# Row halves in turn, transposes, an RMS root on ScalarE and held LayerNorm sums in a two-layer hybrid decoder step

## The chip, the cores and the metric

The kernel runs on one core of a Trainium2 chip. A core has TensorE (PE, with its weight loads as PEld), VectorE (DVE), ScalarE (ACT) and GpSimd (POOL), and SyncE (SP), which here only issues DMAs. The metric is the device time of one execution in microseconds; the median of several runs counts.

## The reference, cut to what matters

One step of a decoder with two layers, in fp32: 1024 new tokens of one prompt, and 32 sample tokens (8 sequences of 4) with states of their own. A layer is a projection `x @ w_in`, three groups of mixers side by side (6 heads RWKV-7, 5 heads GLA, 5 heads RetNet, 64 values to a head), an output projection with LayerNorm, then a gated feed-forward part with a convolution of width 3 over the tokens, and again LayerNorm:

```python
p = x @ w_in[l]
p_rw, p_gl, p_rt = _split(p, (RWKV_COLS, GLA_COLS, RET_COLS))
y_a, sh, s_a = _rwkv7_mix(p_rw, ...)
y_b, s_b = _gla_mix(p_gl, ...)          # ends in _rms_heads(o) * norm_w * silu(g)
y_c, s_c = _ret_mix(p_rt, ...)          # ends in _rms_heads(o) * silu(g)
mix = jnp.concatenate([y_a, y_b, y_c], axis=-1) @ w_out[l]
x = _layer_norm(ALPHA * x + mix, ...)
f, cv = _conv_ffn(x, ...)               # (gelu(a) * b) @ w_down
x = _layer_norm(ALPHA * x + f, ...)
```

with `_rms_heads(o) = o * rsqrt(mean(o * o, -1) + 1e-6)` for each head and token. RWKV's recurrence over tokens (a state of 64 x 64 per head, decayed, corrected and added to) is worked out in chunks of 64 tokens, which takes products within a chunk and the inverse of a unit triangular matrix.

## The kernel before, in words

**Tokens and operands.** The 1056 tokens stand in three blocks `NB` of 384, 384 and 288 columns, channels in the partitions; the third holds the 32 sample tokens and the last 256 of the prompt. Each fp32 weight and activation of the large products is split in a high and a low part (`split`: the high part by a copy on ACT, the low part by a subtraction on POOL), and `mm3` makes three matmuls of each product (high with high, high weight with low activation, low weight with high activation). Small products in the mixers are plain fp32 matmuls, which the trace shows as two instructions each. All matmuls are issued by line L128, all transposes by L131, so groups of the profile are told apart by their tiles.

**Order on TensorE.** A planner, `Tensor`, keeps its instructions in the order in which they are written out. `run` takes streams (generators) and fillers: each burst of a stream ends with a `yield` of the time after which its next burst is expected to have its operands, from the hand-set table `AFTER`; while no stream is ready by the planner's own clock, the filler's matmuls are written out. The engine then follows this order, ready or not: where a time in the table is too short, the engine waits at that burst with the filler behind it. The other engines' orders come from the program's order and the framework's scheduler.

**A layer's stages** (layer 0 / layer 1 in us of the trace):

- First projection tiles and small operands (0 to 95 / 1690 to 1830). `group_a` makes RWKV's 12 M-tiles `pa` of each block by `gemm_steps`, with weights that come in pieces of 256 KB through a `Feed`, `MS = [2, 0, 1, ...]` first.
- RWKV (95 to 590 / 1830 to 2285). For batches `s.b` of 128 tokens (two chunks), eight in a layer, and the samples: `rwkv_front` makes the operands (two small projections `zw`, `za` of 64 rows each, with `sh` from the rows 0 to 63 and 64 to 127), `rwkv_gram` the products within chunks (tile `gps`, operands `ra`, `bk`; a head is 64 rows, a pair of heads 128), `rwkv_tok` the token-major operands (tiles `tv`, `tb`), `rwkv_solve` the triangular inverse on DVE with transfers `gd`, `ud` (lines L630, L632), `rwkv_merge` the joining of its blocks (tiles `xps`, `tps`, copy `x11` at L656), `rwkv_core` the chunk after chunk recurrence (`sp`, `zy`, `up`). Filler is `pa`, and then `group_b`, the projection `gt` for GLA and RET in token tiles.
- GLA, RET and the output projection (590 to 930 / 2285 to 2640). For each of nine token tiles `gla_front`, `gla_back`, `ret_front`, `ret_back`; each back ends in `finish`, which makes the RMS norm and the gate. `out_proj` makes the tiles `po`, adds the residual, and takes LayerNorm's sums as it goes; `LayerNorm.stats` ends them by two matmuls `lnm`, `lnv` and a root by Ln and Exp (L956, L957), `LayerNorm.steps` applies them (subtraction L965, multiplication L966, scale L967) and splits the result into `x1`.
- Feed-forward (930 to 1690 / 2640 to 3385). `up_blocks(0, ...)` makes the first pair of tiles (`wU0` and `wU22`) block by block, since `x1` of the third block comes last; after it `up` and `down` for the other tiles. `up_conv` brings a tile `pu` through the convolution.

The PSUM pool `pm` (tag "m") has two banks for all small RWKV products, `front` in the GLA and RET stage gives banks of a shared tag, and `pd` holds the banks "d" of the down projection.

In `rwkv_gram` each head of the pairs has a bank and a burst of its own:

```python
for j0, j1 in ((0, 2), (2, 3)):
    for h in range(2):
        hs = slice(h * 64, h * 64 + 64)
        gps = pmt("gps")[:, 0:(j1 - j0) * 256].rearrange("p (j c t) -> p j c t", j=j1 - j0, c=2)
```

In `finish` the root is `rsqrt`: 12 small DVE operations on tiles `nw` (128 x 5) by Newton's steps (L242 to L248).

Of the kernel before, what the change touches and what calls it, by code (L numbers as in the profile page):

```python
# [14 lines left out]
ALU = mybir.AluOpType  # L15
# [19 lines left out]
# expected times (us) from a step to what it makes ready  # L35
AFTER = {"key": 5.93, "sh": 3.5, "rkv": 2.0, "block": 6.0, "blockin": 2.5, "x": 3.0, "operands": 8.0, "gram": 0.9, "tv": 0.9, "tb": 0.9, "solve": 24.0, "ud": 4.5, "joined": 4.0, "mask": 1.5, "gd": 4.5, "x11": 1.28, "x21": 1.4, "x22": 0.6, "z": 1.4, "s": 1.58, "am": 2.0, "sx": 1.0, "sout": 3.0, "y": 7.3, "gate": 1.4, "state": 2.5, "done": 7.0, "turn": 2.5, "tokin": 3.36, "ev": 2.25, "gexp": 2.6, "gqt": 1.6, "rrot": 5.5, "rqt": 2.0, "at": 2.5, "qm": 0.8, "vx": 0.9, "gstate": 1.2, "tk": 4.5, "gateout": 4.0, "yin": 2.2, "yout": 4.5, "gnext": 1.2, "rout": 8, "rnext": 0.8, "yt": 0.5, "yready": 1.79, "ln": 3.0, "lnk": 1.5, "lns": 3.0, "ln1": 3.0, "ln2": 9.0}
# [18 lines left out]
# constant columns  # L55
# [10 lines left out]
class Event:  # L66
    """A time on the tensor engine from which something it has to wait for is expected."""
# [7 lines left out]
class Stream:  # L75
    """Work on the tensor engine in bursts: yields the time (us) until the next one can start, or an Event or a condition."""
# [24 lines left out]
class Tensor:  # L101
    """The tensor engine, its instructions kept in the order of the program, with an estimate of its time (us)."""

    def __init__(self, tc, engine):
        self.tc, self.engine, self.t, self.last, self.posts = tc, engine, 0.0, None, []
        Event.clock = self.clock
# [4 lines left out]
    def order(self, ins, cols, passes):  # L111
        ins = ins.ins
# [20 lines left out]
    def post(self, after, do):  # L133
        """Calls `do` when the time has come: a store that would hold up its queue before."""
# [7 lines left out]
    def run(self, streams, filler):  # L142
        """Emits the streams, the first ready one first, and the filler where none is; ends with the streams."""
# [14 lines left out]
def step_kernel(ctx: ExitStack, tc: tile.TileContext, xT, wA, wB, wO, wU, wD, pp, pb, lora, bg, bgk, shT, cvT, srw, sgl, srt,  # L158
# [27 lines left out]
    def split(dst_h, dst_l, src, le=None):  # L186
        """The two parts of src; returns the instructions."""
        return A.copy(dst_h, src), (le or G).tensor_tensor(dst_l, src, dst_h.bitcast(F32), ALU.subtract)  # L188
# [14 lines left out]
    class Feed:  # L203
        """Weights in two parts, piece after piece ([P, k, c] each), as far ahead as there is room."""
# [28 lines left out]
        def k(self, first, k):  # L233
            """The parts of row k of the matrix whose first piece is `first`, and whether its piece ends with it."""
# [3 lines left out]
    def rsqrt(pl, x, mul, add):  # L238
        """1 / sqrt(x * mul + add), by Newton's steps from the exponent's half."""
# [16 lines left out]
    def xtiles(what, n):  # L256
        """The two parts of a block; before the high part of the third one there is room for the low parts of its samples."""
# [4 lines left out]
    def gemm_ch(w, xs, n, name):  # L262
        """One M-tile of channel-major output over block n."""
        ps = pg.tile([P, 512], F32, tag="g", name=name)[:, :NB[n][1]]
# [1411 lines left out]
```

## Time and profile before

| | |
|---|---|
| median of 3 runs | 3442.24 us (3440.7 to 3452.11) |
| span of the profiled execution | 3430.9 us |
| the median over this span | 11.3 us more |
| busy: PE, DVE, ACT, POOL | 93%, 60%, 42%, 39% |
| mean granted clock of TensorE | 0.952 |
| layer 0: RWKV; GLA, RET and output projection; feed-forward | 95 to 590; 590 to 930; 930 to 1690 us |
| layer 1: the same | 1830 to 2285; 2285 to 2640; 2640 to 3385 us |
| last LayerNorm | 3385 to 3431 us |
| DMA | 288.24 MB, mean 84 GB/s |

The profiled execution's only time is its span; the runs are timed from outside it. PE's busy share counts matmuls whose ends are modelled and that overlap, so where one burst ends is read from the start of the next one. A wait in square brackets is idle time of the engine ahead of that instruction, with what ended it. "PE gps L128 <- DVE bk L533" reads: TensorE, about to start a matmul into gps, waited for DVE's write of bk.

### The profile page before, as it was taken

To read this page: it belongs to the slowest core of one execution; us is meant where nothing else is said; L and a number is where in the kernel's file an instruction comes from. 1 tells how busy PE (TensorE), PEld (TensorE's weight loads), DVE (VectorE), ACT (ScalarE), POOL (GpSimd) and SP (SyncE) were. 2 spreads that over 40 slices of the span, in tenths; PEclk is the share of its full clock that TensorE was granted. 3 is DMA by queue.
4 is the path that set the end of the run, shared out by engine and by line. 5 is a ranking of instruction groups with operands and counts; after the bars stand their busy time and mean duration, and the time that the engine had idled before them with its cause. 6 is when DMAs were issued, how large, how long until landed. Compare 5 with 4: busy or idle time off the path is not lost.

```text
span 3430.9 us, 59397 instructions
## 1 busy us (share of the span) xinstructions
PE 3198.4 (93%) x22110; PEld 2975.9 (87%) x22110; DVE 2068.6 (60%) x5037; ACT 1434.7 (42%) x3208; POOL 1332.6 (39%) x1660
## 2 busy tenths in 40 slices
PE   9889999988899999999888999999788999999995
PEld 8778888776799999999877888887777999999995
DVE  3577565776756544454746866646777564545457
ACT  6554332334543334333575543323346423333335
POOL 5443222224553334333565522221336433433345
PEclk9789999998999999999998999999989999999998
DMA  7333213433311111111154432234433111111111
GB/s 249 112 110 99 79 54 102 139 115 102 106 60 47 44 44 50 50 44 50 56 164 140 133 91 68 63 128 119 129 94 100 48 44 44 56 44 44 44 44 56
DMA packets 233261, 288.24 MB, mean 84 GB/s; under 512 B 65212, under 2 KB 146908, under 8 KB 232972
## 3 DMA queue, kind: packets, MB, share of 16 engines
q1 hardware_dynamic: 223852, 271.98, 26.3%
q10 hardware_dynamic: 9120, 12.47, 1.2%
q8 instruction: 173, 2.83, 0.4%
q14 instruction: 116, 0.95, 0.1%
HBM read 225.94 MB, written 58.43 MB: 83 GB/s over the span
## 4 chain that ended last, share of the span: by engine, by line
PE 70%; DVE 16%; DMA 4%; ACT 4%; issue 3%; POOL 2%; SPq 1%; ACTq 0%; DVEq 0%; POOLq 0%
PE pu L128 27%; PE pd L128 13%; PE gt L128 9%; PE pa L128 5%; PE po L128 3%; DVE tm L630 2%; DVE U L632 2%; PE zy L128 2%; PE gps L128 2%; PE rop L128 1%; DVE c L1401 1%; PE gop L128 1%; POOL wil L188 1%; DMA N<-gd 1%; DVE s L940 1%
## 5 line engine op out<-in xcount | busy, mean ns | idle before, releaser
L1401 DVE SCALAR_TENSOR_TENSOR c<-u,ppt,c 128x32 f32<-128x32 f32 (+1 forms) x704 | 395.8, 589 | 545.5 <-ACT c L1392 523.8
L188 POOL TENSOR_TENSOR wil<-wir,wih 128x512 fp32r<-128x512 f32 (+1 forms) x264 | 366.3, 1395 | 365.8 <-ACT wih L188 361.2
L128 PE MATMUL gt<-wih,xh 128*128 128x320 f32 (+1 forms) x1008 | 340.1, 339 | 0.9 <-DVE mx L388 0.9
L1448 DVE TENSOR_TENSOR acc<-acc,pd 128x384 f32<-128x384 f32 (+1 forms) x480 | 247.7, 518 | 139.5 <-PE pd L128 137.5
L128 PE MATMUL gt<-wil,xh 128*128 128x320 f32 (+1 forms) x1008 | 316.1, 315 | 6.5 <-POOL wil L188 5.2
L128 PE MATMUL gt<-wih,xl 128*128 128x320 f32 x896 | 281.6, 314 | 0.0
L188 ACT CAST wih<-wir 128x512 fp32r<-128x512 f32 (+1 forms) x296 | 185.6, 637 | 162.4 <-PE po L128 71.5
L128 PE MATMUL pa<-xh,wih 128*128 128x384 f32 (+1 forms) x576 | 216.5, 376 | 20.4 <-DVE mx L388 11.8
L630 DVE TENSOR_TENSOR tm<-U,N 96x60 f32<-96x60 f32 (+24 forms) x558 | 179.1, 321 | 69.9 <-DMA N<-gd 48.4
L128 PEld LDWEIGHTS gt<-wih,xh 128*128 128x128 f32 (+1 forms) x1008 | 187.5, 186 | 38.6 <-issue 21.9
L128 PE MATMUL pa<-xl,wih 128*128 128x384 f32 (+1 forms) x576 | 201.4, 350 | 3.3 <-POOL xl L188 3.0
L128 PE MATMUL pa<-xh,wil 128*128 128x384 f32 (+1 forms) x576 | 200.7, 348 | 3.6 <-POOL wil L188 2.2
L128 PEld LDWEIGHTS gt<-wil,xh 128*128 128x128 f32 (+1 forms) x1008 | 188.5, 187 | 10.2 <-POOL wil L188 9.1
L188 POOL TENSOR_TENSOR hl<-c,hh 128x384 fp32r<-128x384 f32 x132 | 128.1, 971 | 159.6 <-ACT hh L188 133.0
L632 DVE TENSOR_TENSOR U<-U,tm 96x60 f32<-96x60 f32 (+24 forms) x558 | 170.3, 305 | 14.0
L128 PEld LDWEIGHTS gt<-wih,xl 128*128 128x128 f32 x896 | 173.1, 193 | 0.0
L1392 ACT ACTIVATE c<-pu,ppt 128x384 f32<-128x384 f32 (+1 forms) x264 | 172.8, 655 | 0.0
L1380 ACT COPY u<-pu 128x384 f32<-128x384 f32 x176 | 84.1, 478 | 195.2 <-PE pu L128 195.1
L188 ACT CAST hh<-c 128x384 fp32r<-128x384 f32 x132 | 64.4, 488 | 222.4 <-DVE c L1407 222.3
L128 PEld LDWEIGHTS pa<-xh,wih 128*128 128x128 f32 x576 | 119.7, 208 | 35.1 <-DVE mx L388 13.2
L128 PE MATMUL po<-yh,wih 128*128 128x384 f32 (+1 forms) x384 | 138.9, 362 | 9.1 <-DVE ac L1325 6.7
L128 PE MATMUL po<-yh,wil 128*128 128x384 f32 (+1 forms) x384 | 131.7, 343 | 3.7 <-DVE wil L188 3.7
(810 smaller groups left out, 9862.6 us busy)
## 6 DMA issues: line engine op xcount, KB each, us to landing
wir<-in_wA_dram SPq DMA_DIRECT2D x144, 256.0 KB
wir<-in_wO_dram SPq DMA_DIRECT2D x96, 256.0 KB
wir<-in_wB_dram SPq DMA_DIRECT2D x56, 320.0 KB
tokd<-ev SPq DMA_DIRECT2D x112, 160.0 KB
x<-rkvd SPq DMA_DIRECT2D x16, 576.0 KB
tk<-tokd SPq DMA_DIRECT2D x16, 480.0 KB
rkvd<-mx SPq DMA_DIRECT2D x36, 192.0 KB
tk<-tokd SPq DMA_DIRECT2D x16, 400.0 KB
```

Of the source, the lines that this page charges most:

```text
L128: self.order(self.engine.matmul(out, lhsT, rhs, start=start, stop=stop), cols, 4 if rhs.dtype == F32 else 1)
L188: return A.copy(dst_h, src), (le or G).tensor_tensor(dst_l, src, dst_h.bitcast(F32), ALU.subtract)
L630: V.tensor_tensor(tm, U[:, 0:nr, i:i + 1].to_broadcast([4 * ns, nr, 31 - i]), N[:, i:i + 1, i + 1:32].to_broadcast([4 * ns, nr, 31 - i]), ...
L632: V.tensor_tensor(U[:, 0:nr, i + 1:32], U[:, 0:nr, i + 1:32], tm, ALU.add)
L940: self.ends["V"] = V.tensor_tensor(self.s1, acc[0] if k == 1 else self.s1, acc[k], ALU.add)
L1380: A.copy(u[:, 2:386], ps)
L1392: A.activation(c[:, :W], ps, AF.Identity, scale=pc(PP_CV + 4 * t + 2), bias=pc(PP_CV + 4 * t + 3))
L1401: V.scalar_tensor_tensor(cv, src, pc(PP_CV + 4 * t + tap), cv, ALU.mult, ALU.add)
L1448: V.tensor_tensor(acc[n][m], acc[n][m], ps, ALU.add)
```

## The change

It has seven parts. (1) Small matmuls on 64 rows are written out so that rows 0 to 63 and rows 64 to 127 alternate, each half into a bank of its own: `zw` and `za` in `rwkv_front`; the two heads of a pair in `rwkv_gram`, whose four bursts of a batch become two; and RET's products `rsp`, which took all 128 rows with zeroed copies of the other head before. For these the two scaled copies to `qT` on ACT become part of one copy. (2) `rwkv_tok` makes `tv` (and the samples' `tb`) by transposes instead of matmuls with the identity. (3) `finish` takes the root on ACT by Ln and Exp, with a table load for the set that has both, kept behind Square; the 12 DVE operations go. (4) The first two `pa` tiles of block 0 in a layer are made together, k by k. (5) The third block's LayerNorm sums are built as before but written out (`TE.hold`) only behind the two feed-forward tiles of block 0, and these two take banks of `pd`. (6) In `LayerNorm.steps`, with a split asked for, the odd channels' multiplication goes to POOL and the low part's subtraction to DVE; even channels stay as they were. (7) `AFTER["x11"]` goes from 1.28 to 3.0, and the operands of batches 0 and 1 get 5.5 more.

```diff
-"x11": 1.28,
+"x11": 3.0, "early": 5.5,
...
+    def hold(self, do):
+        self.held = []
+        do()
+        held, self.held = self.held, None
+        return lambda: [self.order(*h) for h in held]
...
+    def gemm_two(feed, first, xs, n, names):
+        ps = [pg.tile([P, 512], F32, tag="g", name=name)[:, :NB[n][1]] for name in names]
+        xh, xl, _ = xs[n]
+        for k in range(KD):
+            for i, p in enumerate(ps):
+                h, lo, _ = feed.k(first + 2 * i, k)
+                mm3(p, h, lo, xh[:, k], xl[:, k], k == 0, k == KD - 1)
+            for _ in range({3: 1, 7: 3}.get(k, 0)):
+                feed.free()
+            if k < KD - 1:
+                yield 0
+        return ps
...
-            for i, z in enumerate((zw, za)):
-                for j in range(NPAIR):
+            for j in range(NPAIR):
+                for i, z in enumerate((zw, za)):
...
-            yield AFTER["operands"]
+            yield AFTER["operands"] + (AFTER["early"] if s.b < 2 else 0)
...
                 for j0, j1 in ((0, 2), (2, 3)):
+                    gps = [pmt("gps")[:, 0:(j1 - j0) * 256].rearrange(...) for _ in range(2)]
+                    for j in range(j0, j1):
+                        for c in range(2):
+                            for h in range(2):
+                                hs = slice(h * 64, h * 64 + 64)
+                                TE.matmul(gps[h][:, j - j0, c], bk(j, c)[hs], ra(j, c)[hs], start=True, stop=True)
                     for h in range(2):
-                        hs = slice(h * 64, h * 64 + 64)
-                        gps = pmt("gps")[:, 0:(j1 - j0) * 256].rearrange(...)
-                        for j in range(j0, j1):
-                            for c in range(2):
-                                TE.matmul(gps[:, j - j0, c], bk(j, c)[hs], ra(j, c)[hs], start=True, stop=True)
-                        V.tensor_tensor(g5[:, j0:j1, :, h], gps, ...)
-                        yield AFTER["gram"]
+                        V.tensor_tensor(g5[:, j0:j1, :, h], gps[h], ...)
+                    yield 2 * AFTER["gram"]
...
-                TE.matmul(tv[:W, j * P:(j + 1) * P], s.v[:, j], ident, start=True, stop=True)
+                TE.transpose(tv[:W, j * P:(j + 1) * P], s.v[:, j], ident)
...
-                    (V if hl or k % 2 else G).tensor_tensor(a, a, s2, ALU.mult)
+                    ((G if k % 2 else V) if hl else (V if k % 2 else G)).tensor_tensor(a, a, s2, ALU.mult)
...
-                        for ins, e in zip(split(hl[0][:, k], hl[1][:, k], a), "AG"):
+                        for ins, e in zip(split(hl[0][:, k], hl[1][:, k], a, V if k % 2 else G), "AV" if k % 2 else "AG"):
...
-            A.activation(sq, dst, AF.Square)
+            first = A.activation(sq, dst, AF.Square)
...
-            sm = rsqrt(gp_, sm, 1.0 / 64, 1e-6)
+            ins = TE.after(A.preload_act_table_set("natural_log_exp_and_others"), first)
+            TE.after(A.activation(sm, sm, AF.Ln, scale=1.0 / 64, bias=eps(1, rows)), ins)
+            A.activation(sm, sm, AF.Exp, scale=-0.5)
...
-            A.copy(qT[:, 0:2], tp[:, 0:2 * rows].rearrange("p (g t) -> p g t", g=2))
-            for h in range(2):
-                A.activation(qT[:, 2 + h:6:2], tp[:, 2 * rows:4 * rows].rearrange(...), AF.Copy, scale=C("h2")[:, h:h + 1])
+            A.copy(qT[:, 0:4], tp[:, 0:4 * rows].rearrange("p (g t) -> p g t", g=4))
...
+            sp = [front("rsp")[:rows, 0:(3 - i) * rows].rearrange(...) for i in range(2)]
             for h in range(4):
-                TE.matmul(sp[:rows, h * rows:(h + 1) * rows], qT[:, 2 + h], qT[:, h // 2], start=True, stop=True)
+                hs = slice((h % 2) * 64, (h % 2) * 64 + 64)
+                TE.matmul(sp[h % 2][:, h // 2], qT[hs, 2 + h // 2], qT[hs, h // 2], start=True, stop=True)
...
-            ln.stats()
+            if n < 2:
+                ln.stats()
+            else:
+                stats3.append(TE.hold(ln.stats))
...
+            ps = gemm_ch(w, x1, n, f"pu{t}", None if t % NJ or n else pd.tile([P, 512], F32, tag="d", name="pu"))
...
+                if n == 0 and j == 0:
+                    stats3[0]()
```

Three places show how the order moves. The first is TensorE in layer 0, at the first gram of the first batch; `pa` with `xh`, `xl` (the activation's parts) and `wih`, `wil` (the weight's parts) is filler. Before:

```order
L128 MATMUL gps<-ra,bk 128x128 x4
L128 MATMUL pa_1_1084<-xh_222,wih_1009 128x384
L128 MATMUL pa_1_1084<-xl_223,wih_1009 128x384
L128 MATMUL pa_1_1084<-xh_222,wil_1008 128x384
L128 MATMUL pa_1_1084<-xh_222,wih_1009 128x384
L128 MATMUL pa_1_1084<-xl_223,wih_1009 128x384
L128 MATMUL pa_1_1084<-xh_222,wil_1008 128x384
L128 MATMUL gps<-ra,bk 128x128 x4
```

Two bursts of four matmuls, each in one bank, with six filler matmuls between them. After, with the numbers of the buffers:

```order
L138 MATMUL pa7_1_1134<-xh1_210,wil36_1051 128x384
L138 MATMUL gps_1155<-ra_898,bk_899 128x128
L138 MATMUL gps_1156<-ra_898,bk_899 128x128
L138 MATMUL gps_1155<-ra_898,bk_899 128x128
L138 MATMUL gps_1156<-ra_898,bk_899 128x128
L138 MATMUL gps_1155<-ra_898,bk_899 128x128
L138 MATMUL gps_1156<-ra_898,bk_899 128x128
L138 MATMUL gps_1155<-ra_898,bk_899 128x128
L138 MATMUL gps_1156<-ra_898,bk_899 128x128
L138 MATMUL pa7_1_1134<-xh1_210,wih37_1071 128x384
```

The eight stand in one burst and alternate between two banks; the first of them is now the 460th matmul of the program, and was the 429th; the first gram of batch 1 goes from the 569th to the 642nd.

The second is ACT at the first `finish` of a GLA tile in layer 0; `yg` is the tile's result, `rsq` its squares, `rsm` their sums by head, `ev` an eviction of the filler's bank `gt`, `upe` one of the state's update. Before:

```order
L981 COPY yg<-gop 128x320
L983 ACTIVATE rsq<-yg 128x320
L876 COPY ev<-gt 128x320
L1076 ACTIVATE upe<-gup,eb 128x64
L1076 ACTIVATE upe<-gup,eb 32x64
```

After:

```order
L1012 COPY yg<-gop 128x320
L1014 ACTIVATE rsq<-yg 128x320
L1018 ACT_TABLE_LOAD
L1019 ACTIVATE rsm<-rsm,cs 128x5
L1020 ACTIVATE rsm<-rsm 128x5
L904 ACT_TABLE_LOAD
L904 ACTIVATE ev<-gt 128x320
L1110 ACTIVATE upe<-gup,eb 128x64
```

Between the squares and the two evictions stand a table load, Ln on what DVE has summed, Exp and a second table load. The program has 118 table loads after the change and had 65; 36 of them are at L1018.

The third is TensorE where layer 0's feed-forward part begins; `po` is the output projection's last tile, `pu` the up projection's tiles with the activation parts `x1h`, `x1l`. Before:

```order
L128 MATMUL po_10249<-yh_9555,wih_10207 128x288
L128 MATMUL po_10249<-yl_9556,wih_10207 128x288
L128 MATMUL po_10249<-yh_9555,wil_10206 128x288
L128 MATMUL lnm<-s_9920,cs 128x288
L128 MATMUL lnv<-s_9921,cs 128x288
L128 MATMUL pu_10404<-x1h_9250,wU0h_10382 128x384
L128 MATMUL pu_10404<-x1l_9251,wU0h_10382 128x384
```

After:

```order
L138 MATMUL pu<-x1h_9166,wU22h_10166 128x384
L138 MATMUL pu<-x1l_9167,wU22h_10166 128x384
L138 MATMUL pu<-x1h_9166,wU22l_10165 128x384
L138 MATMUL lnm<-s_9686,cs 128x288
L138 MATMUL lnv<-s_9687,cs 128x288
L138 MATMUL pu_10240<-x1h_9676,wU0h_10148 128x384
L138 MATMUL pu_10240<-x1l_9677,wU0h_10148 128x384
```

The two LayerNorm matmuls stood right behind the last `po`; now the 48 matmuls of both tiles of block 0 stand ahead of them, and block 1's tiles behind them.

More of the change, by code (lines that the diff above doesn't have):

```diff
@@ L104, in __init__ @@
     def __init__(self, tc, engine):
-        self.tc, self.engine, self.t, self.last, self.posts = tc, engine, 0.0, None, []
+        self.tc, self.engine, self.t, self.last, self.posts, self.held = tc, engine, 0.0, None, [], None
         Event.clock = self.clock
@@ L111, in order @@
     def order(self, ins, cols, passes):
+        if self.held is not None:
+            self.held.append((ins, cols, passes))
+            return
         ins = ins.ins
@@ L433, in group_a @@
             o, W = NB[n]
-            later = []
+            later, two = [], []
             for q, m in enumerate(MS):
                 j, i = divmod(m - 3, 3)
-                ps = yield from gemm_steps(feed, 2 * (n * NA + q), xs, n, f"pa{m}_{n}", True)
+                if n == q == 0:
+                    two = yield from gemm_two(feed, 0, xs, n, [f"pa{i}_{n}" for i in MS[:2]])
+                if two:
+                    ps = two.pop(0)
+                else:
+                    ps = yield from gemm_steps(feed, 2 * (n * NA + q), xs, n, f"pa{m}_{n}", True)
                 key = m == 2 or m > 3 and i == 1
@@ L542, in rwkv_gram @@
             if s.smp:
-                for h in range(2):
-                    hs = slice(h * 64, h * 64 + 64)
-                    gps = pmt("gps")
-                    for j in range(NPAIR):
-                        TE.matmul(gps[:64, j * 64:(j + 1) * 64], bk(j)[hs], ra(j)[hs], start=True, stop=True)
-                    V.tensor_tensor(s.gm[:64, :, h * 64:(h + 1) * 64], gps[:64, 0:192].rearrange("p (j t) -> p j t", j=NPAIR),
+                gps = [pmt("gps") for _ in range(2)]
+                for j in range(NPAIR):
+                    for h in range(2):
+                        hs = slice(h * 64, h * 64 + 64)
+                        TE.matmul(gps[h][:64, j * 64:(j + 1) * 64], bk(j)[hs], ra(j)[hs], start=True, stop=True)
+                for h in range(2):
+                    V.tensor_tensor(s.gm[:64, :, h * 64:(h + 1) * 64], gps[h][:64, 0:192].rearrange("p (j t) -> p j t", j=NPAIR),
                                     C("rkmask_s", 64).unsqueeze(1).to_broadcast([64, NPAIR, 64]), ALU.mult)
@@ L581, in rwkv_tok @@
                 for j in range(NPAIR):
-                    TE.matmul(tb[:64, j * P:(j + 1) * P], bk(j), ident, start=True, stop=True)
+                    TE.transpose(tb[:64, j * P:(j + 1) * P], bk(j), ident)
                 A.copy(s.bkt[:64, :, 0:P], tb[:64, 0:384].rearrange("p (j t) -> p j t", j=NPAIR))
@@ L1152, in ret_front @@
             mk = C("smask" if smp else "retmask", rows)
-            sp = front("rsp")
+            sp = [front("rsp")[:rows, 0:(3 - i) * rows].rearrange("p (h t) -> p h t", t=rows) for i in range(2)]
             for h in range(4):
-                TE.matmul(sp[:rows, h * rows:(h + 1) * rows], qT[:, 2 + h], qT[:, h // 2], start=True, stop=True)
-            s4 = front("rs4")[:rows, 0:rows]
-            TE.matmul(s4, qT[:64, 7], qT[:64, 6], start=True, stop=True)
-            V.tensor_tensor(at[:, 0:4], sp[:rows, 0:4 * rows].rearrange("p (h t) -> p h t", t=rows),
-                            mk.unsqueeze(1).to_broadcast([rows, 4, rows]), ALU.mult)
-            V.tensor_tensor(at[:, 4], s4, mk, ALU.mult)
+                hs = slice((h % 2) * 64, (h % 2) * 64 + 64)
+                TE.matmul(sp[h % 2][:, h // 2], qT[hs, 2 + h // 2], qT[hs, h // 2], start=True, stop=True)
+            TE.matmul(sp[0][:, 2], qT[:64, 7], qT[:64, 6], start=True, stop=True)
+            for i in range(2):
+                V.tensor_tensor(at[:, i:5:2], sp[i], mk.unsqueeze(1).to_broadcast([rows, 3 - i, rows]), ALU.mult)
         def ret_back(s, tt, dst):
@@ L1326, in out_proj @@
                 ln.add(m, V if n == 2 else G)
-            yield AFTER["ln"]
-            ln.stats()
+            yield AFTER["ln"] if n < 2 else 0
+            if n < 2:
+                ln.stats()
+            else:
+                stats3.append(TE.hold(ln.stats))
             x1[n] = xtiles("x1", n)
@@ L1338, in out_projs @@
                 yield from out_proj(n)
+        stats3 = []
         ln1, ln1_at = [None] * 2, [Event() for _ in range(2)]
```

15 lines of the change are left out of this document (7 added, 8 removed).

## The prediction

> **What bounds the kernel now.** I read the page first (span, busy time, chain), then a table by stage, then the waits of TensorE, then single bursts in the timeline. From the page:
>
> ```profile
> span 3430.9 us, 59397 instructions
> PE 3198.4 (93%) x22110; PEld 2975.9 (87%) x22110; DVE 2068.6 (60%) x5037; ACT 1434.7 (42%) x3208; POOL 1332.6 (39%) x1660
> PE 70%; DVE 16%; DMA 4%; ACT 4%; issue 3%; POOL 2%; SPq 1%; ACTq 0%; DVEq 0%; POOLq 0%
> ```
>
> TensorE is busy 93% of the span and carries 70% of the chain that ended last, DVE 16%. That is an average over unlike stages. The table by stage has the stretch, its length, busy time and instructions of PE, PEld, DVE, ACT and POOL, the granted clock, the DMA share and GB/s:
>
> ```profile
> 95.00:200.00 105.00, 88.69 (x497) 78.29 (x499) 64.90 (x163) 53.84 (x118) 49.56 (x54) 0.76 0.41 119
> 200.00:590.00 390.00, 371.02 (x3153) 324.58 (x3154) 253.14 (x940) 147.97 (x344) 114.33 (x118) 0.94 0.29 82
> 590.00:930.00 340.00, 293.39 (x2204) 248.78 (x2203) 242.92 (x568) 136.25 (x355) 118.09 (x100) 0.92 0.40 122
> 930.00:1690.00 760.00, 757.50 (x4708) 754.92 (x4706) 406.85 (x722) 286.49 (x607) 312.10 (x481) 1.00 0.16 48
> 1830.00:2285.00 455.00, 427.26 (x3569) 373.97 (x3568) 309.21 (x1095) 189.99 (x437) 153.49 (x161) 0.94 0.33 93
> 2285.00:2640.00 355.00, 304.91 (x2280) 260.85 (x2279) 246.08 (x582) 148.39 (x381) 123.12 (x109) 0.92 0.38 117
> ```
>
> The feed-forward stretch (930 to 1690) has TensorE busy 757.5 of 760 us at clock 1.00: nothing to gain there but from its first microseconds. The RWKV stretches (95 to 590 and 1830 to 2285) leave 35.3 and 27.7 us without a matmul; the GLA and RET stretches (590 to 930 and 2285 to 2640) 46.6 and 50.1 us. And the clock is 0.76 to 0.94 there. Of the four longest stretches that pull it down, 68.3 us in all, the first and the last in the same view:
>
> ```profile
> 96.20:116.70 20.50, 17.33 (x56) 14.52 (x57) 6.04 (x10) 6.19 (x13) 8.28 (x9) 0.50 0.42 118
> ...
> 219.10:236.20 17.10, 17.10 (x102) 13.81 (x103) 8.83 (x33) 5.59 (x12) 5.06 (x6) 0.50 0.37 100
> ```
>
> All four lie early in layer 0's RWKV stage, at clock 0.50; where matmuls bound it, half of the 68.3, 34 us, are lost. The waits of TensorE that the change touches (us in total, times, longest), and the first of them in the timeline:
>
> ```profile
> PE lnm L128 <- DVE s L940: 23.4, 5, 6.7
> PE tps L128 <- ACT x L656: 16.3, 6, 4.9
> PE gps L128 <- DVE bk L533: 12.5, 5, 6.0
> 99.37 2.07 PE L128 MATMUL gps<-ra,bk 64*128 64x128 f32 x8 [6.01 <-DVE bk L533]
> ```
>
> The first gram matmuls wait 6.01 us for their operands, and the 20.5 us at half clock lie around this wait. The planner had put them there too early, ahead of filler in the in-order queue.
>
> **Row halves and transposes.** Bursts in the timeline (start, length, operation, instructions); two instructions are one fp32 matmul:
>
> ```profile
> 414.57 1.16 PE L128 MATMUL gps<-ra,bk 64*128 64x128 f32 x8
> 415.66 0.94 PE L128 MATMUL xps<-cs,gm 32*32 32x32 f32 x24
> 417.17 0.71 PE L128 MATMUL gps<-ra,bk 64*128 64x128 f32 x4
> 417.80 0.41 PE L128 MATMUL gt<-wih,xh 128*128 128x320 f32 x1
> 435.07 0.60 PE L128 MATMUL zw<-sh,lorat 64*128 64x128 f32 x3
> 435.62 0.27 PE L128 MATMUL za<-sh,lorat 64*128 64x128 f32 x1
> 435.62 0.27 PE L128 MATMUL zw<-sh,lorat 64*128 64x128 f32 x1
> 436.26 0.42 PE L128 MATMUL gt<-wih,xh 128*128 128x320 f32 x1
> 422.77 0.94 PE L128 MATMUL tv<-cs,v 128*128 128x128 f32 x6
> 423.55 0.81 PE L128 MATMUL gp<-bgt,sh 128*128 128x384 f32 x2
> 425.13 0.66 PE L131 MATMUL tb<-cs,bk 128*128 128x128 f32 x4
> 425.54 0.39 PE L128 MATMUL gt<-wih,xh 128*128 128x320 f32 x1
> 693.83 1.16 PE L128 MATMUL rsp<-rqT 128*128 128x128 f32 x8
> 695.34 1.08 PE L128 MATMUL gop<-sgs,qm 32*32 32x64 f32 x16
> ```
>
> Eight gram instructions hold the engine 1.09 us (414.57 to 415.66), four 0.63: 0.115 each and 0.17 for the burst. A zw and a za, one on the upper and one on the lower rows, start together at 435.62: two row halves into two banks run side by side. So a gram batch, now 2 x 1.09 + 2 x 0.63 = 3.44 us, becomes two bursts of eight and four steps, 1.09 + 0.63 = 1.72; over eight batches of prompt tokens in each layer, 16 x 1.72 = 27 us. zw and za take 1.19 us (435.07 to 436.26); six steps are 0.86; 18 x 0.33 = 6. tv takes 0.78 (422.77 to 423.55) in six instructions; four transposes take 0.41, so three 0.31, and 18 x 0.47 = 8. rsp with its fifth head takes 1.51 (693.83 to 695.34); four paired steps and two single ones are 0.86, so 18 x 0.65 = 12. Sum 53 us of TensorE time; bounds 53 and 14 (only the transposes and zw). Also, the two gram banks are now asked for at once where the pool holds two, so a burst waits for both multiplies of the burst before: 0 to 16 x 0.69 = 11 us (at most one eviction's length, near the chance that filler stands between); I take +6. On the path: RWKV is 95% TensorE from 200 to 590, but its chain also runs through DVE and DMA, so three quarters of 41, -31; rsp stands in a stage with 14% idle, half of 12, -6. Together -37, beside the +6.
>
> **Later first grams and x11.** The new numbers put more projection filler ahead of the gram of batches 0 and 1 (about 31 and 73 matmuls further down in the order) and of the first join. That work must run anyway, so a filled wait is a gain, unless the later solve makes something else late: the chain of eight batches begins 5 us later. The wait rows above hold 12.5 + 16.3 = 28.8 us and the half clock 34. Bounds 0 (all moves on to the join) and -63. I take three fifths of the waits, -17, and just over half of the clock, -19: -36.
>
> **RMS root.** All work on tile nw in the GLA and RET stage of layer 0 (length, DVE busy, instructions), groups of the reduction ahead of it and of the multiply behind it, the longest piece of it on the chain, and a table load now in LayerNorm with the activation after it:
>
> ```profile
> 590.00:930.00 340.00, 69.94 (x234) 0.92 0.40 122
> L985 DVE TENSOR_REDUCE rsm<-rsq 128x5 f32<-128x320 f32 (+1 forms) x36 | 17.2, 477 | 4.4 <-ACT rsq L983 4.4
> L989 DVE TENSOR_TENSOR yg<-yg,nw 128x320 f32<-128x320 f32 (+1 forms) x18 | 10.1, 559 | 0.4
> 756.94 4.98 DVE nw L243
> 933.26 1.28 ACT L957 ACT_TABLE_LOAD   x1
> 934.55 0.45 ACT L957 ACTIVATE s<-s 128x288 f32<-128x288 f32 x1
> ```
>
> 234 instructions are 18 tiles of 13, one of them the last multiply (0.56 each, 10 us): 60 us of DVE a layer goes, 25% of DVE's 243 there. One of them stood 4.98 us on the chain. In its place ACT gets for each tile a load of 1.29 us (933.26 to 934.55), Ln, Exp, and, most times, a load back for the next Exp or Tanh. The program's order has 118 table loads for 65: 53 x 1.29 = 68 us, and 36 x 2 small activations of about 0.25 (an estimate from the 0.45 of 288 columns) 18 us more, so 43 us a layer onto ACT's 136 of 340 (40% to 53%). The load lies beside the reduction (0.48), and the tile's own way is some 1.3 + 0.5 against 3 at best and more when DVE is crowded. What could be lost: ACT is in order, so behind an Ln that waits for the reduction stand the copies that free the banks of gt, gop and gup. Bounds -25 a layer (half of the stage's idle time) and +10; I take -11, nearer the gain because DVE, not ACT, is what TensorE waits for there: -22.
>
> The Trainium skill, page "ScalarE: Activation LUTs", section "What ACT_TABLE_LOAD costs", puts a switch of tables at about 1283 ns and a drain of about 1380 ns more, 2.66 us in all. The row above agrees with the first part and shows nothing of the second, since the next activation starts 1.29 us after the load. By the Trainium skill's page the change would put 53 x 2.66 = 141 us on ACT (an estimate), and by the row 68; with 141 the slower rival below gains.
>
> **Held LayerNorm sums, first tiles, other parts.** The sums' wait in the timeline, the matmuls behind it on the chain, POOL's low parts of the third block, and the multiplies of LayerNorm:
>
> ```profile
> 927.46 1.33 PE L128 MATMUL lnm<-s,cs 128*128 128x288 f32 x2 [6.57 <-DVE s L940]
> 929.75 21.36 PE pu L128 x120
> 939.82 4.82 POOL L188 TENSOR_TENSOR x1l<-ac,x1h 128x288 fp32r<-128x288 f32 x6 [0.46 <-ACT x1h L188]
> L966 POOL TENSOR_TENSOR acc<-acc,s 128x384 f32<-128x384 f32 (+1 forms) x12 | 19.9, 1690 | 19.5 <-ACT s L957 19.5
> L966 DVE TENSOR_TENSOR ac<-ac,s 128x384 f32<-128x384 f32 (+1 forms) x48 | 30.4, 679 | 8.0 <-ACT s L957 7.9
> ```
>
> The sums wait 6.57 us before the feed-forward stage; now two tiles of block 0 (48 matmuls of the 0.178 us that the 120 on the chain take, 8.5 us) run first. But the third block's x1l is ready only at 944.6, some 15 us after the sums, and of the tiles ahead of it only block 1's two are left, some 8 us: the wait moves to block 2. Bounds 0 and -6.6 a layer; -1.5 each, -3. Two first pa tiles together: nothing at the start of layer 0, where pieces come by DMA, -3 in layer 1; bounds +2 and -5. The multiply of odd channels of LayerNorm on POOL (1.69 us against 0.68) with the subtraction back on DVE: the 12 or so on the way to x1l lengthen it; bounds -2 and +6; +3.
>
> **Sum.** -37 + 6 - 36 - 22 - 3 - 3 + 3 = -92. From the span 3430.9: 3338.9; the median of runs, 3442.2, lies 11.3 above the span, so 3350.
>
> **Rivals.**
> - *The saved TensorE time turns into waits.* DVE's substitution and the transfers between the batches set RWKV's pace, so shorter bursts only widen the gaps; half of the waits and clock (-18), half of the RMS gain (-11), the small terms (-6): 3442 - 35 = 3407. For it: DVE is 16% of the chain. Against: 95% TensorE from 200 to 590.
> - *Nearly all of the half clock comes back.* 85% of the 53 (-45), 55 of the 63, and -37 for the RMS root with the waits of the GLA stage: 3442 - 137 = 3305. For it: the half-clock stretches follow the very waits that are filled; against: new waits start new ones.
> - *Row halves don't run side by side* in the gram: then the first term is about -7 in place of -37, and the sum 3380. The start at 435.62 speaks against it.
> - *Slower: ACT's in-order queue becomes the bound* of the GLA and RET stage, a load, a wait for the reduction and a load back at each of 36 tiles. 36 x 2.58 = 93 us on the path against the other terms' 70: 3465. It decides once more than 70 / 36 = 1.9 us a tile lands on the path. Against it: ACT stays at about 53%. The drain that the Trainium skill adds to a switch would be what makes it so.
>
> **How the numbers follow.** The forecast 0.50 (its own range 3320 to 3385), waits 0.20, the clock's return 0.17, no overlap 0.06, ACT's queue 0.05, no change at all 0.02. 0.3% is 10 us, about what a measurement of this kernel can tell. Slower is ACT's queue, 0.05; same 0.04 (no change, and the edge of the waits' case); faster 0.91. The range of 3290 to 3415 holds the forecast, most of the waits' case and most of the clock's.
>
> **What would show it.** Right: eight-step gram bursts near 1.1 us with pairs that start together; fewer waits of gps on bk and higher clocks between 95 and 240; no nw rows in GLA and RET, its stretches 10 to 15 us shorter each; the feed-forward stretch unchanged within 3 us, with a wait for x1l at block 2. Wrong: gram bursts still 2 x 1.09; ACT busy over 60% in the GLA stage, with gop or gt waiting for ACT; the waits of tps grown by what gps lost.

## The result, and the profile after

The changed kernel takes 3383.06 us (median of 4 runs, 3381.75 to 3392.01) against 3441.47 before (3440.51 to 3452.11): ratio 0.9839, 95% interval 0.9812 to 0.9866. That is 58 us less where 92 were forecast, and inside the range. The page's span, and its rows of TensorE and of the other engines' busy time, after the change:

```profile
span 3380.6 us, 58890 instructions
PE 3152.3 (93%) x22050; PEld 2928.2 (87%) x22050; DVE 2012.7 (60%) x4605; ACT 1507.0 (45%) x3297; POOL 1338.3 (40%) x1660
```

The spans differ by 50 us. The execution of this profile took 3382.4 us by its own time, 1.8 above its span; so the profiled execution of before, with a span of 3430.9 us, was some 9 us quicker than the median, if its own time lay as little above its span. The 11.3 us that the prediction added at the end were then mostly a spread between runs.

To see where the 50 us come from, each layer is cut at the same events in both traces: the last `zy` of RWKV, the last `po`, the first `pd`. Before, for layer 0 and then layer 1 RWKV with what precedes it, GLA and RET with the output projection, and the way into the feed-forward part (columns as in the prediction's table by stage):

```profile
0.00:574.80 574.80, 529.97 (x4026) 473.68 (x4026) 339.42 (x1128) 266.50 (x587) 209.76 (x230) 0.91 0.38 113
574.80:920.90 346.10, 305.46 (x2263) 255.81 (x2262) 248.71 (x595) 134.77 (x353) 119.42 (x101) 0.93 0.40 122
920.90:977.20 56.30, 49.74 (x293) 48.98 (x294) 35.31 (x55) 33.52 (x70) 33.24 (x48) 0.91 0.25 79
1705.20:2267.70 562.50, 517.13 (x4027) 458.91 (x4027) 356.64 (x1168) 280.73 (x625) 225.31 (x245) 0.94 0.38 109
2267.70:2616.10 348.40, 305.05 (x2270) 255.57 (x2269) 246.67 (x594) 135.05 (x355) 120.42 (x102) 0.93 0.40 121
2616.10:2672.30 56.20, 48.78 (x292) 47.89 (x293) 35.24 (x55) 33.50 (x70) 33.22 (x48) 0.94 0.25 78
```

After, the same stretches:

```profile
0.00:554.90 554.90, 504.50 (x4062) 451.40 (x4062) 345.34 (x1131) 272.30 (x593) 211.16 (x232) 0.95 0.41 120
554.90:886.70 331.80, 301.07 (x2198) 249.92 (x2198) 206.49 (x375) 169.50 (x394) 117.72 (x99) 0.89 0.40 123
886.70:938.40 51.70, 48.74 (x294) 46.78 (x293) 37.25 (x54) 31.07 (x68) 33.42 (x47) 1.00 0.27 82
1670.50:2235.80 565.30, 511.36 (x4046) 454.61 (x4046) 373.27 (x1170) 280.56 (x624) 230.76 (x244) 0.92 0.38 110
2235.80:2570.30 334.50, 294.95 (x2221) 242.81 (x2222) 203.19 (x375) 169.13 (x394) 115.05 (x99) 0.92 0.39 122
2570.30:2622.00 51.70, 48.71 (x294) 46.75 (x293) 37.25 (x56) 30.98 (x68) 34.31 (x47) 1.00 0.26 82
```

And from layer 0's last `po` to the first matmul of layer 1, before and after:

```profile
920.90:1705.20 784.30, 769.40 (x4760) 765.36 (x4760) 428.89 (x759) 298.58 (x631) 321.92 (x489) 0.99 0.16 49
886.70:1670.50 783.80, 769.09 (x4762) 763.81 (x4760) 435.22 (x760) 298.82 (x633) 326.67 (x492) 1.00 0.16 49
```

RWKV is 19.9 us shorter in layer 0 and 2.8 us longer in layer 1; the GLA and RET stage 14.3 and 13.9 shorter, as the prediction's signs had it; the way into the feed-forward part 4.6 and 4.5. Layer 0 gives that back: up to the first matmul of layer 1 only 0.5 us is left of it. In layer 1 it stays (781.4 us before and 777.1 after, from the last `po` to the last `pd`). The forecast had some 61 us for RWKV in both layers (31 and 36 less 6), and 17 came. In the GLA and RET stage DVE's work fell by 42 and 43 us and ACT's rose by 35 and 34.

The stages can't be read alone, because the filler `gt` is one fixed lot for both. Work on tile `gt` on TensorE up to the last `zy` of each layer, of 1456 matmuls a layer, before:

```profile
0.00:574.80 574.80, 181.93 (x1044) 0.91 0.38 113
1705.20:2267.70 562.50, 179.92 (x1037) 0.94 0.38 109
```

After:

```profile
0.00:554.90 554.90, 193.20 (x1110) 0.95 0.41 120
1670.50:2235.80 565.30, 193.96 (x1086) 0.92 0.38 110
```

So RWKV also holds 66 and 49 matmuls more of filler, some 10 and 7 us (an estimate, from the 0.15 us between the starts of two of them); the GLA and RET stage has that much less to do. Counted with it, RWKV gained 30 us in layer 0 and 5 in layer 1. The 17 us can't simply be taken off the 28 in GLA and RET: TensorE has idle time in that stage, and with the RMS root undone and the same filler left, the two stages are 23 us longer (below).

The gram burst in the timeline after, at the place that waited 6.01 us before:

```profile
106.71 1.16 PE L138 MATMUL gps<-ra,bk 64*128 64x128 f32 x16
107.80 0.45 PE L138 MATMUL pa<-xh,wih 128*128 128x384 f32 x1
110.87 1.31 PE L138 MATMUL gps<-ra,bk 64*128 64x128 f32 x8 [0.71 <-DVE gm L590]
```

Sixteen instructions hold the engine 1.09 us (106.71 to 107.80), where eight did before: the row halves run side by side, and the wait for bk is gone. But the second burst now waits for its banks. Two rows of TensorE's waits before (us in total, times, longest):

```profile
PE gps L128 <- DVE gm L559: 2.7, 2, 1.8
PE gp L128 <- ACT gm L666: 1.8, 1, 1.8
```

And after, with others that are read below:

```profile
PE rsp L138 <- ACT qT L1077: 11.7, 4, 5.6
PE gps L138 <- DVE gm L590: 11.6, 6, 4.3
PE gp L138 <- ACT gm L697: 10.5, 5, 3.0
PE lnm L138 <- DVE s L971: 9.9, 3, 6.4
PE ups L138 <- ACT x L692: 7.2, 3, 4.0
PE pu L138 <- POOL x1l L198: 1.8, 2, 0.9
```

The 28.8 us of gps for bk and tps for x11 are gone from the list; gps for gm, gp for gm and ups for x, some 5 us before (0.8 of it ups), are 29 now. `gp` and `ups` stand in the joining chain and its bank "q", just behind the steps whose waits were filled.

### The profile page after: what moved, and what is told of

The parts are those of the page before. It is cut to its first block, busy times and chain, and to the rows that moved or that the text cites. A ratio compares the mean times of both kernels' runs of the same rounds, so it can differ in the third digit from the quotient of the medians.

```text
span 3380.6 us, 58890 instructions
## 1 busy us (share of the span) xinstructions
PE 3152.3 (93%) x22050; PEld 2928.2 (87%) x22050; DVE 2012.7 (60%) x4605; ACT 1507.0 (45%) x3297; POOL 1338.3 (40%) x1660
## 5 line engine op out<-in xcount | busy, mean ns | idle before, releaser
L138 PE MATMUL gt<-wih,xh 128*128 128x320 f32 (+1 forms) x1008 | 349.1, 348 | 4.6 <-DVE mx L412 4.6
L138 PE MATMUL gt<-wil,xh 128*128 128x320 f32 (+1 forms) x1008 | 324.5, 323 | 4.9 <-POOL wil L198 4.9
L138 PE MATMUL pa<-xh,wih 128*128 128x384 f32 (+1 forms) x576 | 208.1, 361 | 25.3 <-ACT wih L198 12.8
```

The costliest lines, as they stand in the source:

```text
L138: self.order(self.engine.matmul(out, lhsT, rhs, start=start, stop=stop), cols, 4 if rhs.dtype == F32 else 1)
```

## The experiments

All were timed against the kernel before, five rounds each. The changed kernel itself was timed once more, to tell parts of 10 us.

> The changed kernel itself, beside the kernel before on the chip that the next three run on, so that parts of some 10 us can be told: a ratio of 0.984 again. The parts taken out so far gave ratios of 0.9886 (numbers), 0.9900 (gram), 0.9861 (tv) and 0.9927 (root); if this one comes to 0.987, tv is worth nothing, numbers and gram some 5 and 10 us.

Ratio 0.9840 (0.9801 to 0.9878), median 3379.1 us, single runs 3368 to 3397. Its profile has a span of 3367.9, 12.7 less than the first, with the same order of instructions. Layer 0's GLA and RET stage here:

```profile
549.40:871.20 321.80, 288.58 (x2198) 239.86 (x2199) 205.51 (x375) 169.42 (x394) 118.49 (x99) 0.94 0.41 126
```

321.8 us at clock 0.94, against 331.8 at 0.89 above: ten microseconds between two executions of one program, with the clock. So a part is told by its ratio, not by one trace, and differences of ratios under about 0.0035 (12 us, from intervals of about 0.002 to 0.004 to either side) mean little. The runs come from three chips, on which the kernel before had medians of 3429 to 3436 us, so differences of medians between chips can be off by some 7 us; a_again, p_cost, n_hold and b_numbers shared one.

| label | what differs from the changed kernel | ratio to before (95%) | median us |
|---|---|---|---|
| a_again | nothing | 0.9840 (0.9801 to 0.9878) | 3379.1 |
| n_numbers | x11 and the early operands as before | 0.9886 (0.9865 to 0.9908) | 3391.0 |
| n_gram | gram as before | 0.9900 (0.9874 to 0.9925) | 3395.0 |
| n_tv | tv, tb by matmuls | 0.9861 (0.9837 to 0.9885) | 3381.9 |
| n_rms | root on DVE | 0.9927 (0.9905 to 0.9949) | 3404.7 |
| n_hold | sums not held | 0.9845 (0.9814 to 0.9875) | 3383.9 |
| n_rsp | RET products as before | 0.9830 (0.9808 to 0.9851) | 3375.8 |
| n_two_vg | first tiles and LayerNorm as before | 0.9876 (0.9853 to 0.9899) | 3388.1 |
| p_cost | planner's costs corrected | 0.9908 (0.9874 to 0.9941) | 3404.6 |
| p_gram | gram 1.8 | 0.9925 (0.9907 to 0.9942) | 3408.0 |
| p_gram_less | gram 0.45 | 0.9894 (0.9863 to 0.9924) | 3395.3 |
| b_numbers | the kernel before with the numbers alone | 0.9953 (0.9933 to 0.9973) | 3419.9 |

**The planner's numbers.** Theory: filling the two waits gains 36 us. Rival: the later solve gives it back.

```diff
-"x11": 3.0, "early": 5.5
+"x11": 1.28, "early": 0.0
```

> The changed kernel with the planner's numbers of before (x11 1.28, nothing added to the operands of batches 0 and 1). If the later first grams and joins gain as forecast (-36), undoing them gives 3383 + 36 = 3419, with waits of gps for bk of some 6 us back in the first 100 to 145 us. The stages of the two traces allow less: first gram 7.3 us later and first zy 4.8 earlier in layer 0, and 3.6 in layer 1, so 8 or so: 3391. Rival: the numbers only delay the chain of batches, and without them the kernel is faster, 3370 to 3380.

> The kernel before with the two planner's numbers alone (x11 3.0, 5.5 more for the operands of batches 0 and 1). As forecast, 36 us faster, a ratio of 0.9895. By what taking the numbers out of the changed kernel cost (8 to 15 us): 0.996. Rival: they gain only with the shorter bursts, 1.000.

0.9886, and 0.9953 alone on the kernel before: 16 us by both ratios, 12 by the medians of the first pair. A gain, and less than half of 36. Without the numbers the waits are back:

```profile
PE gps L138 <- DVE bk L562: 12.0, 4, 5.3
PE tps L138 <- ACT x L687: 10.7, 3, 5.2
```

In the kernel before with the numbers alone (b_numbers) both waits are gone, and the next steps of the chain wait in their place:

```profile
PE ups L128 <- ACT x L661: 20.3, 7, 5.9
PE gp L128 <- ACT gm L666: 10.1, 5, 5.3
PE gps L128 <- DVE gm L559: 6.3, 4, 2.4
```

These three are 36.7 us, and were 5.3 without the numbers, for the 28.8 us that went. In the changed kernel the numbers bring less of it: gps and gp for gm wait 13.0 and 12.0 us there even without them, so of the 29 us only the 7.2 of ups came with the numbers. And what they gain stands in the next stage. With them RWKV holds 94 and 88 matmuls of `gt` more and is 6 and 8 us longer, and the GLA and RET stage, 344.7 and 341.5 us without them, is 13 and 7 shorter.

**The gram.** The edit puts the four bursts of the kernel before back into `rwkv_gram`:

```diff
-gps = [pmt("gps")... for _ in range(2)]
-for j ...: for c ...: for h in range(2): TE.matmul(gps[h][:, j - j0, c], ...)
-yield 2 * AFTER["gram"]
+for h in range(2):
+    gps = pmt("gps")...
+    for j ...: for c ...: TE.matmul(gps[:, j - j0, c], ...)
+    yield AFTER["gram"]
```

> The changed kernel with the gram of before (four bursts a batch, one head and one bank each). The trace shows that the alternation saves 30 us of TensorE slots (66.6 to 36.9). If this time comes back as waits of the next bursts and half clock (the return theory), undoing it costs 10 us or less: 3383 to 3393. If it is kept and the loss lies elsewhere: three quarters of 30, 3405, or more.

0.9900: 16 us by the medians (a_again's and this), 21 by the ratios, between the two expectations. The bursts had saved 30 us of TensorE time (66.6 to 36.9 us of slots over both layers), so half to two thirds of that arrived, the price of the banks included. With the old bursts the wait for the banks falls and another rises:

```profile
PE ups L138 <- ACT x L691: 19.1, 6, 7.0
PE gps L138 <- DVE gm L589: 4.3, 2, 2.4
```

**The transposes.**

```diff
-TE.transpose(tv[:W, j * P:(j + 1) * P], s.v[:, j], ident)
+TE.matmul(tv[:W, j * P:(j + 1) * P], s.v[:, j], ident, start=True, stop=True)
```

> The changed kernel with tv (and the samples' tb) by matmuls with the identity again, 10 us more of TensorE slots (4.9 to 14.9). Return theory: the waits of gp for ACT's copy into gm (10.5 us after, 1.8 before) shrink by as much, 3383 within 3. Kept: 3383 + 8 = 3391.

0.9861, median 3381.9: 3 us by the medians and 7 by the ratios, told neither from nothing nor from the 8 expected. The slots of tv go from 4.9 to 11.2 us in this trace (14.9 in the kernel before, where tv bursts were more often followed by gp or stood in a stretch of half clock). The waits of gp for gm go from 10.5 to 5.7 us (9.7 in a_again), as the return theory says. Those of sp for zs are 10.8, but a_again has 9.6 where the first execution had 5.2, so that is no effect of the edit.

**The RMS root.**

```diff
-ins = TE.after(A.preload_act_table_set("natural_log_exp_and_others"), first)
-TE.after(A.activation(sm, sm, AF.Ln, scale=1.0 / 64, bias=eps(1, rows)), ins)
-A.activation(sm, sm, AF.Exp, scale=-0.5)
+sm = rsqrt(gp_, sm, 1.0 / 64, 1e-6)
```

> The changed kernel with the root of the RMS norm by 12 DVE operations again, no Ln, Exp and table loads in finish. The two GLA and RET stages are 28 us shorter after the change. If that is the root alone (the rsp slots sum to 30.4 us now, 29.3 before): 3411. As forecast, 22 for the root: 3405. Rival: the shorter stage comes from the rsp matmuls and the one copy in place of three, and ACT's loads cost what DVE gains: 3383 within 5.

0.9927, clear of the changed kernel's interval: 26 us by the medians, 30 by the ratios, where 22 were forecast for the root. The two stages, with the same filler left to them (1110 and 1086 matmuls of `gt` ahead of them), are 12.1 and 11.2 us longer (22.1 and 7.9 against a_again), and TensorE waits again for the normed tile:

```profile
557.40:901.30 343.90, 301.16 (x2198) 250.32 (x2198) 239.50 (x591) 130.45 (x331) 115.24 (x99) 0.89 0.38 118
2248.70:2594.40 345.70, 302.65 (x2222) 249.35 (x2223) 239.12 (x591) 129.50 (x332) 116.28 (x99) 0.90 0.38 118
PE ytp L141 <- DVE yt L1022: 29.2, 9, 6.7
```

In the changed kernel that wait is 0.7 us in one place.

**RET's products.** The edit puts back the matmuls over 128 rows and the two scaled copies:

```diff
-A.copy(qT[:, 0:4], tp[:, 0:4 * rows]...)
-TE.matmul(sp[h % 2][:, h // 2], qT[hs, 2 + h // 2], qT[hs, h // 2], ...)
+A.copy(qT[:, 0:2], ...)
+for h in range(2):
+    A.activation(qT[:, 2 + h:6:2], ..., AF.Copy, scale=C("h2")[:, h:h + 1])
+TE.matmul(sp[:rows, h * rows:(h + 1) * rows], qT[:, 2 + h], qT[:, h // 2], ...)
```

> The changed kernel with RET's products as before: four matmuls over 128 rows with zeroed copies of the other head, in one bank, and the two scaled copies on ACT. Forecast for this part: 6 us gained, so 0.9858 here. By the slots in the traces (29.3 us before, 30.4 after, since the burst is now held by qT) nothing: 0.984. Rival: the three ACT copies back in a fuller ACT cost more than the matmuls saved, 0.987 or more.

0.9830: this part is worth nothing that can be told, and perhaps costs a little. The burst is shorter by itself (median slot 1.50 us before, 0.93 after), but waits cut it (11.7 us in the list above), and its slots sum to 29.3 before and 30.4 after. The list names ACT's copy into qT, L1077, which is the last reader of `gtp`, a tile of GLA; the burst itself reads rqT. `front` has two banks, the halves now want both within two instructions, and the second is free only when ACT has read `gtp`. Before, the second bank was wanted for the fifth head alone, and that wait (rs for qT) was 1.1 us. The longest of the four, and ACT meanwhile:

```profile
2358.23 1.23 PE L138 MATMUL rsp<-rqT 64*128 64x128 f32 x8 [5.59 <-ACT qT L1077]
2351.70 1.28 ACT L1018 ACT_TABLE_LOAD   x1
2352.99 1.28 ACT L904 ACT_TABLE_LOAD   x1
2354.81 1.28 ACT L1019 ACT_TABLE_LOAD   x1
2356.43 1.28 ACT L1020 ACT_TABLE_LOAD   x1
2358.00 0.18 ACT L1077 COPY qT<-gtp 32x32 f32<-32x32 f32 x1
```

Four table loads stand ahead of that copy, none of which the kernel before had there: the load at L1018 is undone at once for an eviction, and Ln and Exp each load again. With the root on DVE (n_rms) the waits of rsp for qT are 4.8 us, and with RET's products as before (n_rsp) only 1.1 us of rs are left. So two parts of the change met in ACT's queue.

**Held sums.**

```diff
-stats3.append(TE.hold(ln.stats))
+ln.stats()
...
-ps = gemm_ch(w, x1, n, f"pu{t}", None if t % NJ or n else pd.tile(...))
+ps = gemm_ch(w, x1, n, f"pu{t}")
...
-stats3[0]()
```

> The changed kernel with the third block's LayerNorm sums straight behind the output projection again, and all pu tiles in banks of the pool g. The stretch from the last po to the first pd is 4.6 and 4.5 us shorter after the change; if all of it is due to holding, 3383 + 9 = 3392 (ratio 0.003 more than the changed kernel's). As forecast, 3 us. Rival: nothing, since the wait only moves to block 2.

0.9845, 3383.9: 2 to 5 us, not told from nothing. The waits of lnm for s are 23.4 us again, as before the change, against the 9.9 in the list above: of 13.5 us of filled waits, 2 to 5 arrived. In its trace the way from the last `po` to the first `pd` is 4.0 and 3.6 us longer than the 51.7:

```profile
885.30:941.00 55.70, 49.12 (x293) 48.55 (x294) 37.65 (x56) 32.64 (x72) 32.95 (x48) 0.94 0.25 76
2579.10:2634.40 55.30, 48.76 (x293) 48.19 (x294) 37.63 (x56) 32.27 (x71) 32.64 (x48) 0.94 0.25 77
```

**First tiles and LayerNorm's shares.**

```diff
-if n == q == 0:
+if False:
...
-((G if k % 2 else V) if hl else (V if k % 2 else G)).tensor_tensor(a, a, s2, ALU.mult)
+(V if hl or k % 2 else G).tensor_tensor(a, a, s2, ALU.mult)
...
-split(hl[0][:, k], hl[1][:, k], a, V if k % 2 else G), "AV" if k % 2 else "AG"
+split(hl[0][:, k], hl[1][:, k], a), "AG"
```

> The changed kernel with two small parts undone together: the first two pa tiles one after the other, and LayerNorm's multiplications all on DVE with all low parts on POOL. Forecast: -3 and +3 for these, so no difference, 0.984 within 0.001. If the shared work on POOL and DVE shortened the way to x1l, 3 to 6 us slower: 0.985 to 0.986; the stretch from the last po to the first pd then is longer than 51.7 us.

0.9876, 9 us by the medians and 12 by the ratios; the edge of what can be told, and beyond the larger expectation. Its way to the first `pd` is 3.0 and 3.6 us longer:

```profile
869.90:924.60 54.70, 50.90 (x292) 48.36 (x291) 36.06 (x55) 31.04 (x69) 33.66 (x48) 0.97 0.25 80
2569.70:2625.00 55.30, 51.32 (x294) 48.62 (x293) 33.33 (x53) 30.66 (x68) 32.06 (x47) 0.97 0.25 80
```

So on this way the shared work of POOL and DVE gained where I had it lose. But layer 0 gives it back: from its last `po` to the first matmul of layer 1 this kernel takes 782.4 us, the changed one 783.8. Most of the 9 to 12 us therefore stands elsewhere, and whether the first tiles have a part in it stays open; the two were undone together.

**Why saved TensorE time comes back.** The planner's clock still charges the short bursts at the old cost, so it puts less filler behind them than they now leave room for. Theory: more filler fills the new waits. Rival: the chain sets the pace. The edit halves the charge (`half` is set for zw, za, gps and rsp):

```diff
-self.order(self.engine.matmul(...), cols, 4 if rhs.dtype == F32 else 1)
+self.order(self.engine.matmul(...), cols, (2 if half else 4) if rhs.dtype == F32 else 1)
-self.order(self.engine.transpose(out, in_, identity), identity.shape[1], 4)
+self.order(self.engine.transpose(out, in_, identity), identity.shape[1], 2)
...
-TE.matmul(gps[h][:, j - j0, c], bk(j, c)[hs], ra(j, c)[hs], start=True, stop=True)
+TE.matmul(gps[h][:, j - j0, c], bk(j, c)[hs], ra(j, c)[hs], start=True, stop=True, half=True)
```

> The changed kernel with the planner told what the shorter bursts cost: the paired matmuls of 64 rows (zw, za, gps, rsp) and all transposes at half of their cost in its clock (2 passes for 4), nothing else. If saved time comes back as waits because the planner's clock still charges the old cost and so puts too little filler behind these bursts, the waits of gp for gm, gps for gm and sp for zs (27 us together) shrink by half and the time falls by 8 to 20 us. Rival: the waits are set by the chain through ACT and DVE, whose work filler cannot shorten; the same within 5 us, with other waits in their place.

0.9908, 26 us slower by the medians: the theory falls. The filler goes in early and RWKV grows with it. `gt` up to the last `zy`:

```profile
0.00:589.40 589.40, 219.76 (x1270) 0.94 0.40 116
1690.60:2263.80 573.20, 212.99 (x1215) 0.93 0.38 110
```

160 and 129 matmuls more than in the changed kernel, some 24 and 19 us of work, and RWKV 34.5 and 7.9 us longer. The GLA and RET stage, with that much less filler left, is only 15 and 16 us shorter, at clocks of 0.85 and 0.89. The next two change one number, the time between the two bursts of a gram, to more (p_gram) and to less (p_gram_less):

```diff
-"gram": 0.9
+"gram": 1.8
```

```diff
-"gram": 0.9
+"gram": 0.45
```

> The changed kernel with gram 1.8 for 0.9 in the planner's table, so that 3.6 us instead of 1.8 are expected between the two bursts of a batch's gram and more filler stands there. If the waits of gps for gm (10.8 to 11.6 us in all, 2.7 before) are the price of taking both banks at once, they shrink to under 4 and the time falls by 5 to 10 us against the changed kernel's ratio of 0.984: 0.981 to 0.983. Rival: the chain through the solution starts later by what the filler takes, and nothing or less than nothing is left: 0.984 to 0.988, as with the corrected costs (0.9908).

> The changed kernel with gram 0.45 for 0.9, so 0.9 us instead of 1.8 between the two bursts of a batch's gram; with 1.8 (3.6 us) it was slower, 0.9925, though RWKV took 117 and 120 matmuls more of filler in. If the start of each batch's solution sets RWKV's pace, an earlier second burst gains up to 16 x 0.9 = 14 us of chain: 0.980 to 0.983, with less filler done by the end of RWKV and more in the GLA and RET stage. Rival: the second burst only waits longer for its banks, TensorE idles and its clock drops: waits of gps for gm over 15 us and 0.986 to 0.990.

Both are slower: 0.9925 and 0.9894. With 1.8 the waits of gps for gm vanish, as expected, and the gain does not come; those of gp double. With 0.45 the rival is met, the waits of gps for gm growing to over 15 us. One row of p_gram, then one of p_gram_less:

```profile
PE gp L138 <- ACT gm L697: 19.8, 7, 6.0
```

```profile
PE gps L138 <- DVE gm L590: 25.6, 23, 5.9
```

RWKV is 16.7 us longer in layer 0 with 1.8 (571.6, with 117 filler matmuls more, about as much work) and 14.1 shorter with 0.45 (540.8, with 42 filler matmuls less); in layer 1 both are longer (590.2 and 583.2 for 565.3). That layer's stage varies by itself, though: n_rsp, in which TensorE's order there is the changed kernel's, has 575.4. So a filled wait at one step of the chain shows up at the next, and the table as it stands is near a minimum for this number. None of these kernels is faster than the changed one beyond the intervals; n_rsp's 0.9830 is the lowest ratio.

## Why the prediction was right, and where its sum was off

- *Row halves and transposes, -37 + 6.* The TensorE time was as forecast: gram slots 30 us less (forecast 27), zw and za 4.8 (6), tv 10.0 from before to after (8); the two halves run side by side. For the gram the sum had three quarters of 27 less 6 for the banks, 14, and 16 to 21 came, so that share holds. The place of the banks was named rightly: 11.6 us of waits of gps for gm, 8.9 more than before, above the +6 taken and within the 0 to 11. The transposes were to bring 6; 3 to 7 were measured, with 12 of doubt. rsp's 6 did not show: the sum charged the banks for the gram alone, and the same price fell due in `front`.
- *Later first grams and x11, -36.* The waits of 28.8 us went as forecast. The failing step is "a filled wait is a gain": the mis-sized term measured 12 to 16 us. With the numbers alone the waits came back one step on, 36.7 us for 5.3. The clock between the first gram and the first `zy` of layer 0 rose from 0.74 (99.4 to 193.5 us) to 0.90 (106.7 to 188.7 us), but that is not the numbers' alone: it is 0.89 with them alone (101.9 to 185.2) and 0.89 with all but them (102.0 to 177.8).
- *RMS root, -22.* Measured 26 to 30. DVE lost the nw work, some 60 us a layer (42 net), ACT rose by 35 (43 forecast) to 51% of the stage, and ACT's in-order queue did not become the bound. It did make TensorE wait, above all in the rsp bursts shown above. The loads and Ln, as groups after the change:

```profile
L1018 ACT ACT_TABLE_LOAD x36 | 46.2, 1283 | 0.6
L1019 ACT ACTIVATE rsm<-rsm,cs 128x5 f32<-128x5 f32 (+1 forms) x36 | 10.7, 298 | 2.1 <-DVE rsm L1016 1.9
```

  Ln waited 1.9 us in all for DVE's sums: the load lay beside the reduction, as the prediction had it. And the drain of about 1380 ns that the Trainium skill ("ScalarE: Activation LUTs", "What ACT_TABLE_LOAD costs") adds to each switch does not show: in 25 of these 36 places the next operation starts 1.29 us after the load's start, as here, and in 5 more another load does, the one that undoes it.

```profile
645.05 1.28 ACT L1018 ACT_TABLE_LOAD   x1
646.35 0.30 ACT L1019 ACTIVATE rsm<-rsm,cs 128x5 f32<-128x5 f32 x1
```

- *Held sums -3, first tiles -3, LayerNorm's shares +3.* The wait for x1l that was to take the sums' place is 1.8 us in two places, so block 2 was not late. The way into the feed-forward part is 9.1 us shorter in both layers together, of which 4.8 are left at the end of the layers. The held sums' 2 to 5 us agree with the forecast 3. The sign of LayerNorm's shares was wrong on that way; what they and the first tiles are worth in the whole, 9 to 12 us when undone together, is not told apart.
- *From the span to the median, +11.3.* Mostly a spread between runs, as told above. It sets the forecast beside the median and is no part of the -92.

The rival "the saved TensorE time turns into waits" gave 3407, the forecast 3350; 3383 lies between, in a range 125 us wide in which errors of both signs partly offset each other: the numbers came out 20 us short, the root and the last small parts above their forecast. Saved time did turn into waits in RWKV, above all in layer 1, but not for the rival's reason: the waits are for ACT's and DVE's copies and for banks, and the one for the transfers (xps for gm) is 0.3 us. In GLA and RET the forecast's mechanism holds.

Open: how much of the 58 us the half clock has a part in. Two executions of one program differ by 10 us in one stage with it, and it could not be held still. And the parts undone one by one sum to 54 us by the medians against a mean of 3381 and 85 by the ratios, with some 12 us of doubt on each, of which the changed kernel's own ratio, in all of them alike, has some 8: they are not shown to add up, nor not to.

## What to carry to other kernels

Where a hand-set order mixes a chain with a fixed lot of filler, count the filler on both sides of a stage's end before crediting the stage; and credit time saved on the busiest engine only up to the next wait of the chain, since a filled wait reappears one step on. An operation that moves from a crowded engine to one with room, table loads included, kept its whole value here, while faster bursts on the busiest engine kept half to two thirds of theirs (the gram) or nothing that can be told (the transposes, RET's products). Before letting two halves write two banks at once, look who must free the second: it cost waits in both pools of two. Cost figures in a planner that look wrong can still be tuned against the rest of its table: correcting them alone lost 26 us.

## What the runs showed of the hardware

One program, run twice, had granted clocks of 0.89 and 0.94 in the same stage and ten microseconds between them, without another difference in its order. Two fp32 matmul streams on the two row halves, into two banks, took 1.09 us for sixteen instructions where one took 1.08 to 1.09 for eight. A table load of ScalarE took 1.28 us, and in 25 of 36 places the next operation started 1.29 us after the load's start.
